# The last feed-forward product with tokens in the rows: what a change of layout in the final stage of an fp32 two-block transformer kernel does to its time

## The chip, the cores and the metric

The kernel runs on one core of one Trainium2 chip. The metric is device time in microseconds (us); of several runs the median is given. A profile is one execution recorded by the hardware profiler: its span reaches from the first to the last instruction. TensorE is called PE (its weight loads PEld), VectorE DVE, ScalarE ACT, GpSimd POOL, SyncE SP.

## What is computed

256 tokens of 1024 features pass through a first block of two layers (block-sparse attention, gated linear attention, attention into a memory), then 16 learned tokens are put ahead of them and a second block of two layers follows. Each layer of the second block is a feed-forward, a mixer and another feed-forward, each with a norm before and after. What the change touches is the last line of the loop at i = 1, and the return:

```python
def swiglu(h, w1, w3, w2):
    return (jax.nn.silu(h @ w1) * (h @ w3)) @ w2
...
        f = swiglu(rmsnorm(h, ffn_norm_pre[i, 1]), ffn_w1[i, 1], ffn_w3[i, 1], ffn_w2[i, 1])
        h = h + 0.5 * rmsnorm(f, ffn_norm_post[i, 1])
    return h[:, N_META:]
```

`w1` and `w3` are 1024 x 2816, `w2` is 2816 x 1024. All is float32.

## The kernel before

Activations lie with features in the partitions: `h[k]` is 128 features by 272 tokens (16 + 256), k = 0 to 7. A product takes a 128 x 128 block of weights as the stationary operand and streams the tokens past it (272 columns, or 256 where the 16 extra tokens aren't needed, as in the last feed-forward, `lo = 16`). For precision each operand is split into two fp32r parts, hi and lo, and `mm3` (L250) makes three matmuls of one product: lo by hi, hi by lo, hi by hi (L253, L254, L255).

The weights come in the order of one long plan (`full_plan`), eight blocks (a "chunk", 512 KB) to a DMA on SP's queue; ACT casts a chunk to its hi part (L222) and DVE subtracts to get the lo part (L223). Six chunks are held. `take` hands out blocks and lets the next chunk be loaded. A scheduler of the framework then sets the order of the instructions on each engine and puts the waits in.

`ffn` (L958): the first NG = 3 pairs of columns of w1 and w3 are made together with the eight k outside, since `h` becomes ready one k after another; the other 19 pairs follow one by one (`dense`, L478). `act` makes silu(a) * b of each and splits it into `fh[m]`, `fl[m]`, m = 0 to 21. Then the w2 product: for each of eight feature tiles m, 22 blocks by three matmuls of 256 columns into one PSUM bank; `branch_out` (L930) squares the bank on ACT (`fq`, L938), makes a copy times the gain on DVE (`fg`, L939) and sums squares on POOL (L948). After the last tile, matmuls with a matrix of 1/1024 (L956) put the mean of the squares of each token into all partitions.

The end of `second_block` (L1213 to L1222) takes Ln and Exp of that (`t_last`, `s_last`), and for each of the eight tiles a multiplication and an addition of `h` (two tiles on POOL, six on DVE) and a store of 128 KB, by turns from ACT's and SP's queues.

Between a mixer and a feed-forward stands `boundary` (L880): per k, `fg` times the scale (L892), the addition to `h` (L893, L895), the split into `xh[k]` (ACT, L352) and `xl[k]` (DVE, L353), a square on ACT (`sq`, two buffers) and a sum of squares on POOL (`acc`, L904). PE waits there for the first `xh`.

Of the kernel before, what the change touches and what calls it, by code (L numbers as in the profile page):

```python
# [8 lines left out]
F32 = mybir.dt.float32  # L9
# [58 lines left out]
DEFER = 12  # L68
AFTER_K = 3
# [38 lines left out]
def plan_ffn(i, j):  # L108
# [8 lines left out]
    p += plan_cols("ffn_w2_2", (i, j), [128 * m for m in range(KD)], KF)  # L117
# [49 lines left out]
class Kern:  # L167
# [82 lines left out]
    def mm3(self, out, a, b, start, stop):  # L250
        """out += a.T @ b from the two parts of each."""
# [5 lines left out]
    def mm3s(self, outs, ws, x, start, stop):  # L257
        """mm3 of several weight blocks with one x, its first part first."""
# [8 lines left out]
    def psum(self, **tags):  # L267
        """Shares out PSUM's banks: each tag's tiles follow one another in trace order."""
# [73 lines left out]
    def rsqrt(self, out, src, eps, n, tmp):  # L342
        """out = (src + eps) ** -0.5"""
        self.nc.scalar.activation(tmp, src, AF.Ln, bias=eps, scale=1.0)
        self.nc.scalar.activation(out, tmp, AF.Exp, bias=0.0, scale=-0.5)
# [9 lines left out]
    def sumsq(self, src, pool, n, tag, eng, qtag="sq"):  # L355
        """sum over the tiles of src of their squares, one tile."""
# [68 lines left out]
    def headnorm(self, dst, src, g):  # L425
        """dst = src * g / rms over each head's features."""
# [9 lines left out]
    def group_norm(self, tiles, gains):  # L436
        """Each of up to four tiles (two heads of 64 features each) over its heads' rms, times its gain."""
# [29 lines left out]
    def sigmoid(self, x):  # L467
        """exp(min(x, 0) - ln(1 + exp(-|x|))), silu's factor of x, by the tables that the norms use."""
# [16 lines left out]
    def mem_kv(self, l):  # L485
        """Keys (not normalised yet) and values of the memory tokens."""
# [26 lines left out]
    def first_layer(self, l):  # L513
# [13 lines left out]
        # inputs of the linear attention  # L527
# [28 lines left out]
        # queries and keys  # L556
# [200 lines left out]
    def gla(self, l, rb, qb, kb, vb):  # L757
# [24 lines left out]
        # states before chunks 1..3  # L782
# [16 lines left out]
        # scores by halving: the exponents never exceed 0  # L799
# [10 lines left out]
        # diagonal: q.k of each token  # L810
# [10 lines left out]
        def prepare(n):  # L821
# [5 lines left out]
            # queries of the four heads side by side, each head's features alone  # L827
# [52 lines left out]
    def boundary(self, fg, pss, g, after, lo=0, cols=False):  # L880
        """Adds the normalised branch to the residual and prepares the next product; returns the scale per
        token that the product carries."""
# [47 lines left out]
    def branch_out(self, ps, m, gpost, c, lo, st, bias=None, direct=1):  # L930
        """Evacuates feature tile m of a branch: its gained copy and its squares."""
# [26 lines left out]
    def ffn(self, i, j, scale, lo=0):  # L958
# [3 lines left out]
        with self.psum(mm=7), self.tc.tile_pool(name=self.nm("ffn"), bufs=1, reuse_waits="tile") as fp:  # L962
# [21 lines left out]
            for m in range(NG, KF):  # L984
                pa = self.dense("ffn_w1_2", self.xh, self.xl, n, KD, lo)
                pb = self.dense("ffn_w3_2", self.xh, self.xl, n, KD, lo)
                act(m, pa, pb)
# [290 lines left out]
```

## Time and profile before

| | |
|---|---|
| median of 3 runs | 1297.11 us (1296.04 to 1300.18) |
| profiled execution, span | 1289.3 us |
| its own time | the page gives no more than the span; the median lies 7.8 us above it |
| PE busy | 1253.6 us, 97% of the span |
| DVE, ACT, POOL busy | 66%, 54%, 17% |
| mean granted clock of PE | 0.992 |
| HBM read, written | 199.64 MB, 1.05 MB |

The busy time of PE is an upper bound of its work, since matmuls are pipelined and their ends are modelled; what a matmul costs is the distance between the starts of two in a row.

### The profile page before, as it was taken

The page shows a single profiled execution, that of the slowest core. Times are in us where ns is not written, and L with a number is a line of the kernel's source. Part 1 is how long each engine was busy: PE and PEld are TensorE (multiplying, and loading weights), DVE is VectorE, ACT ScalarE, POOL GpSimd, SP SyncE. Part 2 cuts the span into 40 slices and gives each one's busy share as a digit, 9 for nine tenths or more (in the row PEclk, how much of TensorE's full clock was granted, in tenths as well). Part 3 has the DMA queues.
Part 4 walks back from the last instruction along what each step waited for, and adds up shares of the span by engine and source line. Part 5 has one row for each costly group of instructions (what it writes and reads, how often), then busy time and mean ns, then how long its engine had stood idle before and what let it go on. Part 6 is the DMA issues. An engine that isn't in the chain of part 4 may idle for free.

```text
span 1289.3 us, 24664 instructions
## 1 busy us (share of the span) xinstructions
PE 1253.6 (97%) x9812; PEld 1203.9 (93%) x9812; DVE 855.6 (66%) x1431; ACT 694.8 (54%) x1207; POOL 216.3 (17%) x325
## 2 busy tenths in 40 slices
PE   8999999999999999799999999999999999999996
PEld 7888998889999999599999989999999888999996
DVE  7977768677666644786665477665466786866643
ACT  6768657486544443564444465444355665654541
POOL 5101110011311102441111022110120002311111
PEclk9999999999999999899999999999999999999999
DMA  8453553235555555146555536555536333665541
GB/s 297 141 172 106 166 165 99 101 128 169 176 181 178 174 173 178 33 158 186 169 177 179 175 115 205 177 179 169 177 100 194 131 99 99 211 190 188 181 146 34
DMA packets 59955, 202.29 MB, mean 157 GB/s; under 512 B 7488, under 2 KB 11584, under 8 KB 59840
## 3 DMA queue, kind: packets, MB, share of 16 engines
q1 hardware_dynamic: 59264, 200.19, 48.6%
q8 instruction: 77, 1.26, 0.4%
q10 hardware_dynamic: 576, 0.52, 0.1%
q14 instruction: 38, 0.31, 0.1%
HBM read 199.64 MB, written 1.05 MB: 156 GB/s over the span
## 4 chain that ended last, share of the span: by engine, by line
PE 89%; DVE 3%; ACT 2%; issue 1%; POOL 0%; DVEq 0%; ACTq 0%; POOLq 0%
PE mm L253 24%; PE mm L255 24%; PE mm L254 24%; PE mm L261 2%; PE mm L264 2%; PE mm L262 2%; DVE xl L353 1%; PE mb L253 1%; PE mb L255 1%; PE mb L254 1%; DVE fg L892 1%; PE gl L839 1%; DVE h L895 1%; PE mb L445 1%; PE at L1121 1%
## 5 line engine op out<-in xcount | busy, mean ns | idle before, releaser
L223 DVE TENSOR_TENSOR lo<-raw,hi 128x1024 fp32r<-128x1024 f32 (+1 forms) x376 | 471.9, 1259 | 255.9 <-ACT hi L222 255.2
L222 ACT CAST hi<-raw 128x1024 fp32r<-128x1024 f32 (+1 forms) x376 | 391.0, 1043 | 378.7 <-PE mm L255 353.4
L253 PE MATMUL mm<-xh,lo 128*128 128x272 f32 (+1 forms) x1680 | 484.8, 289 | 0.0
L255 PE MATMUL mm<-xh,hi 128*128 128x272 f32 (+1 forms) x1680 | 481.7, 287 | 0.0
L254 PE MATMUL mm<-xl,hi 128*128 128x272 f32 (+1 forms) x1680 | 481.1, 286 | 0.0
L253 PEld LDWEIGHTS mm<-xh,lo 128*128 128x128 f32 x1680 | 317.0, 189 | 4.2 <-issue 3.6
L254 PEld LDWEIGHTS mm<-xl,hi 128*128 128x128 f32 x1680 | 317.1, 189 | 1.2 <-issue 1.0
L255 PEld LDWEIGHTS mm<-xh,hi 128*128 128x128 f32 x1680 | 317.2, 189 | 0.4 <-issue 0.3
L255 PE MATMUL mm<-fh,hi 128*128 128x272 f32 (+1 forms) x704 | 201.8, 287 | 0.0
L253 PE MATMUL mm<-fh,lo 128*128 128x272 f32 (+1 forms) x704 | 201.4, 286 | 0.0
L254 PE MATMUL mm<-fl,hi 128*128 128x272 f32 (+1 forms) x704 | 201.0, 286 | 0.0
L973 POOL TENSOR_TENSOR a<-a,b 128x272 f32<-128x272 f32 (+1 forms) x88 | 82.8, 943 | 403.2 <-DVE b L972 367.6
L253 PEld LDWEIGHTS mm<-fh,lo 128*128 128x128 f32 x704 | 132.6, 188 | 0.0
L254 PEld LDWEIGHTS mm<-fl,hi 128*128 128x128 f32 x704 | 132.5, 188 | 0.0
L255 PEld LDWEIGHTS mm<-fh,hi 128*128 128x128 f32 x704 | 132.3, 188 | 0.0
L948 POOL TENSOR_TENSOR facc<-facc,fq 128x272 f32<-128x272 f32 (+1 forms) x34 | 31.8, 934 | 322.8 <-ACT fq L938 316.6
L972 DVE TENSOR_TENSOR b<-mm,r 128x272 f32<-128x272 f32 (+1 forms) x88 | 38.3, 435 | 42.6 <-PE mm L255 42.5
L348 ACT CAST fh<-a 128x272 fp32r<-128x272 f32 (+1 forms) x88 | 36.7, 417 | 54.2 <-POOL a L973 54.2
L261 PE MATMUL mm<-xh,lo 128*128 128x272 f32 (+1 forms) x208 | 55.7, 299 | 9.8 <-ACT xh L352 9.8
L262 PE MATMUL mm<-xh,hi 128*128 128x272 f32 (+1 forms) x208 | 54.2, 290 | 0.0
L261 PEld LDWEIGHTS mm<-xh,lo 128*128 128x128 f32 x208 | 40.1, 193 | 11.3 <-ACT xh L352 11.1
L349 DVE TENSOR_TENSOR fl<-a,fh 128x272 fp32r<-128x272 f32 (+1 forms) x88 | 39.0, 443 | 17.3 <-ACT fh L348 17.3
(347 smaller groups left out, 1697.5 us busy)
## 6 DMA issues: line engine op xcount, KB each, us to landing
raw<-in_w_dram SPq DMA_DIRECT2D x372, 512.0 KB, 3.5
h<-in_xt_dram SPq DMA_DIRECT2D x8, 128.0 KB, 5.5
raw<-in_w_dram SPq DMA_DIRECT2D x4, 256.0 KB, 5.8
memt<-in_memt_dram SPq DMA_DIRECT2D x1, 1024.0 KB, 8.5
memt<-in_memt_dram SPq DMA_DIRECT2D x2, 512.0 KB, 4.8
out_dram<-fg ACTq DMA_DIRECT2D x4, 128.0 KB, 1.8
out_dram<-fg SPq DMA_DIRECT2D x4, 128.0 KB, 1.8
vec<-in_vecs_dram SPq DMA_DIRECT2D x1, 336.5 KB, 3.0
```

Source lines behind the costliest of these rows:

```text
L222: nc.scalar.copy(hi[:, s], raw[:, s])
L223: nc.vector.tensor_sub(lo[:, s], raw[:, s], hi[:, s].bitcast(F32))
L253: mm(out, a[1], b[0], start=start, stop=False)
L254: mm(out, a[0], b[1], start=False, stop=False)
L255: mm(out, a[0], b[0], start=False, stop=stop)
L261: mm(out, w[1], x[0], start=start, stop=False)
L262: mm(out, w[0], x[0], start=False, stop=False)
L348: self.nc.scalar.copy(hi, x)
L349: self.nc.vector.tensor_sub(lo, x, hi.bitcast(F32))
L948: nc.gpsimd.tensor_add(R(st["acc"]), R(st["acc"]), R(q))
L972: nc.vector.tensor_mul(b, pb[:, :n], r[:, lo:])
L973: nc.gpsimd.tensor_mul(a, a, b)
```

## The change

The w2 product of the last feed-forward, and it alone, is turned over. The stationary operand is now a 128 x 128 piece of the activations (tokens by features of the middle layer), and 512 columns of weights are streamed past it, so that the result has 128 tokens in the partitions and 512 features in one PSUM bank. There are two halves of the features (b) and two of the tokens (t); in the second half of the features the last four of the 22 steps of k are made for t = 0 first and then for t = 1. The norm after it, the residual and the store follow in that layout: ACT squares with a running sum, DVE multiplies by the gain (a row spread over all partitions, `grow`, loaded by a new DMA and halved on POOL), Ln and Exp work on one column, and one instruction per 128 x 512 piece multiplies by the scale and adds the residual. The residual is `h` transposed by PE, 16 transposes of 128 x 128 in four groups behind the pairs m = 8, 10, 12 and 14, each group copied to SBUF by ACT. The output leaves in four stores of 256 KB. The weights' plan orders the same blocks of w2 to fit; the host passes one more array and no longer transposes the result. Instructions of the changed kernel have line numbers of their own (`mm3` stands at L259 to L261, the split of the weights at L228 and L229).

```diff
+    if (i, j) == (1, 1):
+        for n in range(2):
+            for k in range(KF):
+                p += block("ffn_w2_2", (i, j), k, 512 * n, 512)
+    else:
+        p += plan_cols("ffn_w2_2", (i, j), [128 * m for m in range(KD)], KF)
...
                 act(m, pa, pb)
+                if idx == (1, 1) and m in (8, 10, 12, 14):
+                    self.residual_rows(fp, (m - 8) // 2, lo)
             self.table("natural_log_exp_and_others")
+            if idx == (1, 1):
+                return self.last_rows(fp, fh, fl, lo)
...
+    def residual_rows(self, fp, q, lo):
+        nc = self.nc
+        if q == 0:
+            self.hT = [fp.tile([128, D], F32, name=f"hT{t}") for t in range(2)]
+            self.grow = fp.tile([128, D], F32, name="grow")
+            nc.sync.dma_start(self.grow, self.io["grow"].to_broadcast([128, D]))
+            nc.gpsimd.tensor_scalar(self.grow, self.grow, 0.5, None, op0=OP.mult)
+        b, t = divmod(q, 2)
+        ps = self.bank()
+        for i in range(4):
+            nc.tensor.transpose(ps[:, 128 * i:128 * i + 128], self.h[4 * b + i][:, lo + 128 * t:lo + 128 * t + 128],
+                                self.ident)
+        nc.scalar.copy(self.hT[t][:, 512 * b:512 * b + 512], ps)
...
+    def last_rows(self, fp, fh, fl, lo):
...
+        for b in range(2):
+            c = slice(512 * b, 512 * b + 512)
+            acc = [self.bank() for _ in range(2)]
+            x = lambda t, k: [p[k][:, lo + 128 * t:lo + 128 * t + 128] for p in (fh, fl)]
+            held = KF - LAST_K if b else KF
+            for k in range(held):
+                w = self.take(4, "ffn_w2_2")
+                for t in range(2):
+                    self.mm3(acc[t], x(t, k), w, k == 0, k == KF - 1)
+            ws = [self.take(4, "ffn_w2_2") for k in range(held, KF)]
+            for t in range(2):
+                for k, w in zip(range(held, KF), ws):
+                    self.mm3(acc[t], x(t, k), w, k == 0, k == KF - 1)
+                sq = fp.tile([128, 512], F32, name=self.nm("sqr"), tag="sqr", bufs=2)
+                nc.scalar.activation(sq, acc[t], AF.Square, accum_out=ss[:, 2 * t + b:2 * t + b + 1])
+                f = fg[t][b] = fp.tile([128, 512], F32, name=self.nm("fgr"), tag=f"fgr{t}{b}")
+                nc.vector.tensor_mul(f, acc[t], self.grow[:, c])
+                if b == 0:
...
+                    continue
+                s = ss[:, 6 + t:7 + t]
+                nc.scalar.activation(s, ss[:, 2 * t + 1:2 * t + 2], AF.Ln, bias=ss[:, 4 + t:5 + t], scale=1.0 / D)
+                nc.scalar.activation(s, s, AF.Exp, bias=0.0, scale=-0.5)
+                for d in range(2):
+                    o = fg[t][d]
+                    e = slice(512 * d, 512 * d + 512)
+                    nc.vector.scalar_tensor_tensor(o, o, s, self.hT[t][:, e], op0=OP.mult, op1=OP.add)
+                    (nc.sync if d else nc.scalar).dma_start(self.io["out"][t][:, e], o)
...
-            st = self.ffn(1, 1, r, lo=NMETA)
-            s = t2.tile([128, L2], F32, name="s_last", tag="s")[:, NMETA:]
-            t = t2.tile([128, L2], F32, name="t_last", tag="ms")[:, NMETA:]
-            self.rsqrt(s, st["pss"][:, NMETA:L2], self.eps, S, t)
-            for k in range(KD):
-                f = st["fg"][k][:, NMETA:]
-                eng = nc.gpsimd if k in (2, 5) else nc.vector
-                eng.tensor_mul(f, f, s)
-                eng.tensor_add(f, f, self.h[k][:, NMETA:])
-                (nc.sync if k % 2 else nc.scalar).dma_start(self.io["out"][k], f)
+            self.ffn(1, 1, r, lo=NMETA)
```

**Where the scheduler puts the load and the halving of `grow`.** In the code they stand behind the pair m = 8. On POOL's queue at the `boundary` ahead of the last feed-forward (`facc` are the sums of the attention's branch, `acc` the sums of the boundary) stood before:

```order
L948 TENSOR_TENSOR facc_12935<-facc_12935,fq_13083 128x256 [waits Activation_49,Pool_49]
L948 TENSOR_TENSOR facc_12935<-facc_12935,fq_13088 128x256 [waits Activation_49,Pool_49]
L904 TENSOR_TENSOR acc_13131<-acc_13131,sq_13141 128x256 [waits PE_49,Activation_49]
L904 TENSOR_TENSOR acc_13131<-acc_13131,sq_13148 128x256 [waits Activation_49,Pool_49]
L904 TENSOR_TENSOR acc_13131<-acc_13131,sq_13155 128x256 [waits Activation_49,Pool_49]
```

and now, with SP's queue of the same place behind it (`raw` are the chunks of weights):

```order
L954 TENSOR_TENSOR facc_12935<-facc_12935,fq_13083 128x256 [waits Activation_49,Pool_49]
L954 TENSOR_TENSOR facc_12935<-facc_12935,fq_13088 128x256 [waits Activation_49,Pool_49]
L1012 TENSOR_SCALAR grow<-grow 128x1024 [waits DMAHW4_49,DVE_49]
L910 TENSOR_TENSOR acc_13131<-acc_13131,sq_13141 128x256 [waits PE_49,Activation_49]
L910 TENSOR_TENSOR acc_13131<-acc_13131,sq_13148 128x256 [waits Activation_49,Pool_49]
L910 TENSOR_TENSOR acc_13131<-acc_13131,sq_13155 128x256 [waits Activation_49,Pool_49]
```

```order
L222 DMA raw_13338<-in_w_dram 128x1024 [waits DMAHW4_49,DVE_49]
L222 DMA raw_13362<-in_w_dram 128x1024 [waits DMAHW5_49,DVE_49]
L1011 DMA grow<-in_grow_dram 128x1024 [waits PE_49,Pool_49]
L222 DMA raw_13393<-in_w_dram 128x1024 [waits DMAHW6_49,DVE_49,Activation_49]
L222 DMA raw_13460<-in_w_dram 128x1024 [waits DMAHW7_49,DVE_49,Activation_49]
```

The load has moved ahead of the chunks of the feed-forward, and the halving ahead of the sums of the boundary.

**The end on ACT and DVE.** On DVE's queue behind the last split of weights there stood before fifteen rows: `fg` of three tiles, and six multiplications and six additions (POOL had the other two of each); the last eight were:

```order
L1220 TENSOR_TENSOR fg_2571_15138<-fg_2571_15138,s_last 128x256
L1220 TENSOR_TENSOR fg_2583_15228<-fg_2583_15228,s_last 128x256
L1221 TENSOR_TENSOR fg_2571_15138<-fg_2571_15138,h_76 128x256 [waits DVE_49]
L1221 TENSOR_TENSOR fg_2583_15228<-fg_2583_15228,h_77 128x256 [waits DVE_49]
L1220 TENSOR_TENSOR fg_2598_15390<-fg_2598_15390,s_last 128x256
L1220 TENSOR_TENSOR fg_2601_15462<-fg_2601_15462,s_last 128x256
L1221 TENSOR_TENSOR fg_2598_15390<-fg_2598_15390,h_79 128x256 [waits DVE_49]
L1221 TENSOR_TENSOR fg_2601_15462<-fg_2601_15462,h_80 128x256 [waits DVE_49]
```

Now all that DVE has there, t = 0 and then t = 1 (`mm_15030` and `mm_15031` are the two banks):

```order
L1041 TENSOR_TENSOR fgr_15190<-mm_15030,grow 128x512 [waits Activation_49]
L1052 SCALAR_TENSOR_TENSOR fgr_15022<-fgr_15022,ss_rows,hT_13879 128x512 [waits DVE_49,Activation_49]
L1052 SCALAR_TENSOR_TENSOR fgr_15190<-fgr_15190,ss_rows,hT_13879 128x512 [waits DVE_49]
L1041 TENSOR_TENSOR fgr_15212<-mm_15031,grow 128x512 [waits Activation_49]
L1052 SCALAR_TENSOR_TENSOR fgr_15027<-fgr_15027,ss_rows,hT_13880 128x512 [waits Activation_49]
L1052 SCALAR_TENSOR_TENSOR fgr_15212<-fgr_15212,ss_rows,hT_13880 128x512 [waits DVE_49]
```

and on ACT, where the store of t = 0 stands ahead of the Square of t = 1:

```order
L1039 ACTIVATE sqr_15188,ss_rows<-mm_15030 128x512 [waits PE_49,Activation_49]
L1047 ACTIVATE ss_rows<-ss_rows 128x1 [waits DVE_49,Activation_49]
L1048 ACTIVATE ss_rows<-ss_rows 128x1 [waits Activation_49]
L1053 DMA out_dram<-fgr_15022 128x512 [waits DVE_49]
L1039 ACTIVATE sqr_15210,ss_rows<-mm_15031 128x512 [waits PE_49,Activation_49]
L1047 ACTIVATE ss_rows<-ss_rows 128x1 [waits Activation_49]
L1048 ACTIVATE ss_rows<-ss_rows 128x1 [waits Activation_49]
L1053 DMA out_dram<-fgr_15027 128x512 [waits DVE_49]
```

So behind the last matmul three DVE instructions follow a Square, where twelve followed the Exp; and the ACT queue now holds a store that waits for DVE ahead of the last Square.

## Rows read from the trace of the kernel before

**Rows 1.** The page, part 4: shares of the span in the chain that ended last, by engine.

```profile
PE 89%; DVE 3%; ACT 2%; issue 1%; POOL 0%; DVEq 0%; ACTq 0%; POOLq 0%
```

**Rows 2.** Busy time by engine in the stretch of the last w2 product: stretch, its length, then per engine busy us and count, PE's granted clock, DMA share, GB/s.

```profile
1215.00:1277.50 62.50, 62.50 (x530) 62.50 (x530) 24.82 (x26) 22.02 (x26) 6.33 (x7) 1.00 0.32 102
```

**Rows 3.** Groups by line and shape: one of the three lines of `mm3` in that product; the other two have as many.

```profile
L255 PE MATMUL mm<-fh,hi 128*128 128x256 f32 x176 | 49.6, 282 | 0.0
```

**Rows 4.** PE's instructions in order of time (start, duration, both us): the first and the last of the 528 matmuls of that product.

```profile
1215.29 0.28 PE L253 MATMUL mm<-fh,lo 128*128 128x256 f32 x1
...
1277.68 0.28 PE L255 MATMUL mm<-fh,hi 128*128 128x256 f32 x1
```

**Rows 5.** The same view in the second layer of the first block, where a product with 512 columns of weights moving past activations exists already (values of its attention): first and last of two runs of eleven matmuls without a break.

```profile
254.09 0.40 PE L254 MATMUL mm<-lo,xh 128*128 128x512 f32 x1
...
256.42 0.39 PE L255 MATMUL mm<-hi,xh 128*128 128x512 f32 x1
...
257.93 0.39 PE L254 MATMUL mm<-lo,xh 128*128 128x512 f32 x1
...
260.21 0.40 PE L255 MATMUL mm<-hi,xh 128*128 128x512 f32 x1
```

**Rows 6.** The same view in the attention of the second block: five transposes between two fp32r products.

```profile
1057.04 0.28 PE L255 MATMUL mm<-oh,hi 128*128 128x256 f32 x1
1057.16 0.49 PE L1141 MATMUL at<-ident,e 128*128 128x128 f32 x3
1057.49 0.38 PE L1143 MATMUL at<-ident,e 128*16 128x128 f32 x2
...
1057.95 0.28 PE L255 MATMUL mm<-oh,hi 128*128 128x256 f32 x1
```

**Rows 7.** The chain that ended last, at its end (start, length, what), and behind it, from the instructions in order of time, the issue of the last store.

```profile
1278.05 0.39 ACT fq L938
...
1280.18 1.29 DVE fg L1220 x2
...
1285.73 0.34 DVE fg L1221
...
1286.43 0.33 SPq L1222 DMA_DIRECT2D out_dram<-fg  x1
```

**Rows 8.** Groups by line and shape on ACT: count, then busy us and mean ns of one, then idle time before them. The second is a Square from PSUM, the third what follows each instruction with a running sum.

```profile
L744 ACT COPY pT<-mb 128x512 f32<-128x512 f32 x8 | 4.5, 599 | 1.0 <-PE mb L741 1.0
L938 ACT ACTIVATE fq<-mm 128x256 f32<-128x256 f32 x10 | 3.7, 384 | 20.9 <-PE mm L255 20.9
L688 ACT ACTIVATION_READ_ACCUMULATOR lg<-lg,sm 128x1 f32 x32 | 6.0, 186 | 0.0
L877 ACT ACTIVATE rt<-ss,eps 128x2 f32<-128x2 f32 x1 | 0.3, 262 | 1.7 <-PE ss L919 1.7
L878 ACT ACTIVATE rc<-rt 128x2 f32<-128x2 f32 x1 | 0.2, 193 | 0.0
```

**Rows 9.** The same on DVE, two shapes of 512 columns.

```profile
L829 DVE TENSOR_TENSOR bd<-X,hm 128x512 f32<-128x512 f32 x12 | 8.2, 683 | 0.0
L474 DVE SCALAR_TENSOR_TENSOR sl<-ga,sl 128x512 f32<-128x512 f32 x8 | 6.1, 762 | 2.0 <-ACT sl L473 2.0
```

**Rows 10.** The page, part 6: DMA issues, KB each, median us from issue to landing.

```profile
raw<-in_w_dram SPq DMA_DIRECT2D x372, 512.0 KB, 3.5
...
out_dram<-fg SPq DMA_DIRECT2D x4, 128.0 KB, 1.8
```

**Rows 11.** Instructions in order of time at the `boundary` ahead of the last feed-forward: DVE, ACT and PE up to the first matmul, and DVE beside POOL a little later.

```profile
1086.84 0.42 DVE L892 TENSOR_TENSOR fg<-fg,s 128x256 f32<-128x256 f32 x1 [1.23 <-ACT s L878]
1087.30 0.43 DVE L893 TENSOR_TENSOR h<-h,fg 128x256 f32<-128x256 f32 x1
...
1087.76 0.51 ACT L352 ACTIVATE xh<-h,vec 128x256 fp32r<-128x256 f32 x1 [0.95 <-DVE h L893]
...
1088.32 0.39 PE L261 MATMUL mm<-xh,lo 128*128 128x256 f32 x1 [2.47 <-ACT xh L352]
...
1090.05 1.61 POOL L904 TENSOR_TENSOR acc<-acc,sq 128x256 f32<-128x256 f32 x2 [5.66 <-ACT sq L903]
1090.10 0.97 DVE L895 TENSOR_TENSOR h<-h,fg 128x256 f32<-128x256 f32 x1
```

**Rows 12.** Busy time by engine just behind that first matmul, columns as in rows 2.

```profile
1088.30:1092.40 4.10, 4.08 (x22) 4.09 (x23) 4.10 (x10) 3.09 (x8) 1.87 (x3) 0.59 0.02 4
```

**Rows 13.** SP's two issues of chunks that stand on either side of the new load, and DVE's split of the chunk of the second.

```profile
1081.23 0.33 SPq L216 DMA_DIRECT2D raw<-in_w_dram  x1
...
1096.77 0.33 SPq L216 DMA_DIRECT2D raw<-in_w_dram  x1
...
1106.73 1.23 DVE L223 TENSOR_TENSOR lo<-raw,hi 128x1024 fp32r<-128x1024 f32 x1 [0.80 <-ACT hi L222]
```

**Rows 14.** The only multiplications by a constant on POOL, in the first microseconds of the kernel (group), and one DVE addition ahead of them and one beside them, in order of time.

```profile
L339 POOL TENSOR_SCALAR alibi<-d 128x256 f32<-128x256 f32 x8 | 7.8, 990 | 0.3
...
10.97 0.42 DVE L365 TENSOR_TENSOR acc<-acc,sq 128x256 f32<-128x256 f32 x1
...
12.79 0.62 DVE L365 TENSOR_TENSOR acc<-acc,sq 128x256 f32<-128x256 f32 x1
```

**Rows 15.** Groups by line in the stretch 1215.3 to 1277.5: ACT's casts of weights, and what they waited for.

```profile
L222 ACT CAST hi<-raw 128x1024 fp32r<-128x1024 f32 x17 | 17.8, 1049 | 22.0 <-PE mm L255 22.0
```

More of the change, by code (lines that the diff above doesn't have):

```diff
@@ L68 @@
 DEFER = 12
+LAST_K = 4
 AFTER_K = 3
@@ L116, in plan_ffn @@
         p += plan_cols("ffn_w3_2", (i, j), (128 * m,), KD)
-    p += plan_cols("ffn_w2_2", (i, j), [128 * m for m in range(KD)], KF)
+    if (i, j) == (1, 1):
[4 more added lines that the diff above has]
+        p += plan_cols("ffn_w2_2", (i, j), [128 * m for m in range(KD)], KF)
     return p
@@ new lines, in last_rows @@
+    def last_rows(self, fp, fh, fl, lo):
+        nc = self.nc
+        ss = fp.tile([128, 8], F32, name="ss_rows")
+        fg = [[None] * 2 for _ in range(2)]
+        for b in range(2):
[16 more added lines that the diff above has]
+                if b == 0:
+                    nc.vector.tensor_scalar(ss[:, 4 + t:5 + t], ss[:, 2 * t:2 * t + 1], 1.0 / D, EPS, op0=OP.mult,
+                                            op1=OP.add)
+                    continue
[7 more added lines that the diff above has]
+                    (nc.sync if d else nc.scalar).dma_start(self.io["out"][t][:, e], o)
@@ L1258, in pack @@
         "metat": fm(A["meta_tokens_2"]),
+        "grow": A["ffn_norm_post_2"][1, 1].reshape(1, D),
     }
@@ L1271 @@
         io[name] = nc.dram_tensor(f"in_{name}_dram", a.shape, mybir.dt.from_np(a.dtype), kind="ExternalInput").ap()
-    io["out"] = nc.dram_tensor("out_0_dram", (KD, 128, S), F32, kind="ExternalOutput").ap()
+    io["out"] = nc.dram_tensor("out_0_dram", (2, 128, D), F32, kind="ExternalOutput").ap()
     with _tile.TileContext(nc) as tc:
@@ L1276 @@
     got = r.results[0]["out_0_dram"]
-    return np.ascontiguousarray(np.asarray(got).reshape(D, S).T).reshape(1, S, D)
+    return np.asarray(got).reshape(1, S, D)
```

## The prediction

> **What bounds the kernel now.** I read the shares of the chain that ended last first: 89% of it is PE [rows 1]. So a saving counts only where PE is busy, or where PE waits. Next come the stages. Over the last w2 product PE has no pause, and DVE and ACT work 25 and 22 of 62.5 us [rows 2]; their splits of weights wait for PE, not PE for them [rows 15]. There are 528 matmuls [rows 3], and from the first start to the last are 62.4 us [rows 4], so each takes 62.39/527 = 0.118 us. The duration in such a row (0.28) is latency and prices nothing. Then the end: after the start of the last matmul at 1277.68 the kernel still runs 11.6 us, and the chain there is a Square, matmuls with the mean, Ln, Exp, and six us of DVE, from 1280.18 to 1286.07 [rows 4, 7]. Here PE is idle and everything counts. Last, the boundary ahead of this feed-forward, since the scheduler has put new work there: PE waits for two DVE instructions and one of ACT, until 1288.32 [rows 11].
>
> The profiled span is 1289.3 us, the median of the runs 7.8 us more; I take these 7.8 us as unchanged and count from 1297.1. A measurement of this kernel can tell about 0.3% (3.9 us) from no change.
>
> **1. The product.** 528 matmuls of 256 columns become 264 of 512: as many columns in all. What a matmul of 512 columns takes, with weights moving and activations stationary, stands in the trace: ten steps from 254.09 to 256.42, and ten from 257.93 to 260.21 [rows 5], 0.233 and 0.228. Two of 256 columns take 0.237. I take 0.231, the middle: from first to last start 263 x 0.231 = 60.8 us, **-1.6 us**. Bounds: -2.4 at 0.228, -0.1 at 0.237. Chunks of weights are then wanted every 2.77 in place of 2.84 us; the casts have 22 us of waiting to spare [rows 15], so I cost that at nothing. The first half's Squares and multiplications run beside the second half's matmuls, as `fq` and `fg` did.
>
> **2. The transposes.** 16 of them lie on PE's path. Five in a row put 1057.95 - 1057.04 = 0.91 us between matmuls that otherwise stand three steps, 0.354, apart [rows 6]: 0.111 each, the change from one kind to the other included. 16 x 0.111 = **+1.8 us**. The row's durations (0.49 for three started 0.11 apart, so 0.27 for one) are latency again; if the change paid them it would be 4.4. The lower bound is the same 1.8: the work is new and PE has no gap. The Trainium skill (TensorE: Matmul & The Clock Gate, Part 4: PE-mode transpose) gives about 275 ns for one in a kernel's context; by that figure the estimate would be 4.4 us, the upper bound above. The rows agree with it as a latency and not as a price. ACT's four copies of 512 columns, 0.60 each [rows 8], lie in a stretch where PE isn't waited on by them: the bank they free is wanted seven products later.
>
> **3. The end.** Now, counted from the start T of the last matmul. Before, the Square began 0.37 later [rows 4, 7]; 512 columns stream 0.11 longer, 0.48. A Square of 256 columns takes 0.38, a copy of 512 takes 0.60: I take 0.62, and 0.19 for reading the sum out [rows 8]: T + 1.29. The multiplication by the gain waits for the Square, as `fg` did for `fq`: start at T + 1.33. Ln and Exp on one column (0.26 + 0.19, [rows 8]) lie beside it. DVE then has 0.68 + 0.76 + 0.76 [rows 9], less 0.08 for each overlap of two in a row: T + 3.4. The store of 256 KB lands between the 1.8 us of 128 KB and the 3.5 of 512 KB [rows 10]; by size 2.4: T + 5.8. From the last landing to the end of the span were 1289.3 - 1286.43 - 1.8 = 1.1 us [rows 7, 10]: T + 6.9, against 11.6. **-4.7 us**, with bounds of -5.3 and -3.6 from the two landings. The half t = 0 ends 12 matmuls, 2.8 us, earlier; its store stands on ACT's queue ahead of the last Square and waits for DVE's second instruction: 1.29 + 0.04 + 0.60 + 0.76 = 2.7 us after t = 0's last matmul, and issuing takes 0.33 [rows 7], so ACT is free at about T + 0.2 to 0.3, before T + 0.48. It hides, by 0.2 us.
>
> The eight Squares, `fg` and the sums on POOL of the old product go, and were hidden under PE [rows 2]: nothing.
>
> **4. The boundary.** Load and halving of `grow` stand earlier than in the code. On SP the load stands between the chunks issued at 1081.23 and 1096.77 [rows 13]; the second chunk has another reason for its late issue, so the queue loses nothing. With 3.5 us for 512 KB [rows 10], and a chunk ahead of it in the same queue, `grow` lands between 1085.1 and about 1088.5. POOL then multiplies 1024 columns: four times the 0.99 us of 256 [rows 14] is 4 us at most. It can meet the two DVE instructions on PE's path, 1086.84 to 1087.73 [rows 11]. Beside POOL's multiplications by a constant one DVE addition took 0.62 in place of 0.42 [rows 14]. I take one such 0.2: **+0.2 us**. The lower bound is 0, when `grow` lands after 1087.7: the next instructions have some 2 us of slack, since PE's clock is then at 0.59 of full on average [rows 12], between its levels of 1.2 and 2.4 GHz, and it works off the first k slowly. The upper bound is the first rival.
>
> **Sum:** -1.6 + 1.8 - 4.7 + 0.2 = -4.3 us, 1297.1 - 4.3 = **1292.8 us**. With the bounds of points 1 and 3 this case runs from 1291.4 to 1295.4.
>
> **The rivals.** *DVE is locked out while POOL halves `grow`.* Beside POOL's sums the addition of DVE took 0.97 in place of 0.42: begun at 1090.10, it ended just after POOL's first sum did [rows 11]. If the halving holds DVE off for as long as it runs, 4 us, and begins at 1086.2, DVE's first instruction begins at 1090.2 in place of 1086.84: +3.3 us, 1295.9. For it speak the sums; against it the multiplications by a constant, beside which DVE lost only 0.2 [rows 14], and the chance that `grow` comes too late to matter. The Trainium skill (SBUF — State Buffer, Who interferes with whom) has this as its rule: a DVE instruction with two SBUF inputs and a GpSimd instruction that reads SBUF exclude each other for the whole instruction. The sums of rows 11 agree with that rule, the additions of rows 14 don't. Chance 0.17.
>
> *The transposes are not pipelined* in the midst of this product and cost their latency: +2.6, 1295.4. Against it: they are pipelined between products of the same kind in rows 6. Chance 0.07.
>
> *The stream gains more.* At 0.228 a matmul and a landing of 1.8 us the sum is -5.9: 1291.2. Chance 0.13.
>
> *SP's queue is blocked, and it is slower.* The load of `grow` waits for PE and for POOL. Were the event it waits for one of this feed-forward, in place of one long past, the loads of all its chunks would stand behind it. That decides from the point where the wait outlasts 1096.77 by the spare time of the next chunk, which lands 3.5 us after its issue and is split at 1106.73 [rows 10, 13]: 6.5 us, so from 1103.3. If it waited for its place in the code, behind the pair m = 8 (six pairs of 48 matmuls at 0.118 after PE's first 144, about 1141), PE would lose 38 us: 1335. Against it: the tiles that lay in that memory belong to stages that are over, and the scheduler placed the load ahead of the feed-forward's own. Chance 0.02.
>
> *The change does not do what it says*: 512 columns take exactly twice 256 and the stores land late, so that -0.1 + 1.8 - 3.6 + 0.2 = -1.7 is left: 1295.4. Chance 0.03.
>
> **How the numbers follow.** The forecast has 0.58. Of it a little under two thirds lies under 1293.2, the 0.3% line, which is only 0.4 us away; the faster rival lies there whole: 0.37 + 0.13, and a little of the others, 0.52 for faster. The lock, the dear transposes and the rest of the forecast make 0.45 for no change. Slower by over 0.3% is the blocked queue, with a little for what I don't see: 0.03. The range of 8 in 10 goes from 1290.5 (below the faster rival, by what a median of few runs may lie off) to 1296.2 (above the lock).
>
> **What the profile after would show.** Steps of 0.231 between starts in the w2 product, and about 60.8 us from first to last; four groups of transposes, each holding the next product back by 0.44; from the last matmul to the end of the span 6.9 us, with Square, multiplication and two more DVE instructions in it; `grow`'s halving on POOL between 1085 and 1092, and PE's first matmul of the feed-forward at 1088.5. The forecast is wrong if that first matmul comes after 1090 (the lock), if the steps lie at 0.237 or more, if the last store lands over 3 us after its issue, or if the last Square begins late because ACT still holds the store of t = 0.

## The result and the profile after

The changed kernel takes 1288.49 us (median of 22 runs, 1286.42 to 1297.19) beside 1295.43 for the kernel before (22 runs, 1290.84 to 1300.88): a ratio of 0.9949 [0.9935, 0.9963], so 4.8 to 8.4 us less. The forecast was 1292.8, the range from 1290.5: the sign is right, the time lies 2 us under the range. Where that comes from is followed below: the sum of what the change does in the traces is the one forecast (two of its terms were off and cancelled), and the point it was counted from was not.

The profiled execution of the changed kernel has a span of 1295.5 us and a time of 1297.2, the longest of the 22. So the spans of this profile and of the one before can't be subtracted. Stretches of the two can, where PE's granted clock (the share of its full speed that PE was allowed) is the same. The engines and the chain, from the page:

```profile
PE 1263.2 (98%) x9560; PEld 1200.7 (93%) x9560; DVE 850.9 (66%) x1421; ACT 696.3 (54%) x1213; POOL 214.7 (17%) x316
PE 90%; DVE 2%; ACT 2%; issue 1%; POOL 0%; DVEq 0%; ACTq 0%; POOLq 0%
```

DVE has 2% of the chain where it had 3 [rows 1], as a shorter end would have it; PE's 90% in place of 89 also holds the longer half clock of this execution. The product (PE in order of time: its first and last matmul, then the group of one of its three lines):

```profile
1228.20 0.39 PE L259 MATMUL mm<-hi,fl 128*128 128x512 f32 x1
...
1289.24 0.39 PE L261 MATMUL mm<-hi,fh 128*128 128x512 f32 x1
```

```profile
L261 PE MATMUL mm<-hi,fh 128*128 128x512 f32 x88 | 34.6, 393 | 0.0
```

These answer to [rows 3, 4]: 264 matmuls in 61.03 us, 0.232 a step, where 528 took 62.38. **-1.35 us.** One of the four groups of transposes, in the same view:

```profile
1152.49 0.28 PE L261 MATMUL mm<-xh,hi 128*128 128x256 f32 x1
1152.61 0.60 PE L1016 MATMUL mm<-ident,h 128*128 128x128 f32 x4
1152.96 0.36 PE L259 MATMUL mm<-xh,lo 128*128 128x256 f32 x1
1153.16 0.28 PE L260 MATMUL mm<-xl,hi 128*128 128x256 f32 x1
```

From 1152.49 to 1153.16 are 0.67 us; two steps of 0.118 would be 0.24. So a group costs 0.43 to 0.44, and four cost **+1.76 us** (all four groups are alike). The last 924 matmuls ahead of the product say the same: 109.24 us before, 111.00 after. The end, DVE, ACT and SP in order of time, and the stores from the page:

```profile
1290.38 0.69 DVE L1041 TENSOR_TENSOR fgr<-mm,grow 128x512 f32<-128x512 f32 x1 [0.72 <-ACT sqr L1039]
1290.99 1.41 DVE L1052 SCALAR_TENSOR_TENSOR fgr<-fgr,ss_rows,hT 128x512 f32<-128x512 f32 x2
...
1289.04 0.38 ACTq L1053 DMA_DIRECT2D out_dram<-fgr  x1
1289.66 0.60 ACT L1039 ACTIVATE sqr<-mm 128x512 f32<-128x512 f32 x1 [1.48 <-DVE fgr L1052]
1290.16 0.19 ACT L1039 ACTIVATION_READ_ACCUMULATOR sqr<-mm 128x1 f32 x1
```

```profile
out_dram<-fgr SPq DMA_DIRECT2D x2, 256.0 KB, 2.1
```

Counted from the last matmul, T = 1289.24: Square at T + 0.42, multiplication at T + 1.14, DVE done at T + 3.16 (1290.99 + 1.41), the store issued then lands 2.1 us later, and the span ends at T + 6.24. ACT's wait ahead of the Square is put down to DVE, but ACT had issued t = 0's store by 1289.42: the last matmul set it. Before, it was 11.62 [rows 4, 7]: **-5.38 us.**

Part of that lay in how the kernel before shared its end between DVE and POOL. Two of DVE's additions beside POOL's, and two without:

```profile
1281.39 1.81 DVE L1221 TENSOR_TENSOR fg<-fg,h 128x256 f32<-128x256 f32 x2
1282.01 1.76 POOL L1221 TENSOR_TENSOR fg<-fg,h 128x256 f32<-128x256 f32 x2
...
1285.66 0.75 DVE L1221 TENSOR_TENSOR fg<-fg,h 128x256 f32<-128x256 f32 x2
```

Four of the twelve DVE instructions were lengthened so, by about 0.53 us each, 2.1 in all, while POOL took four instructions off DVE that would have cost it some 0.34 each. By this estimate the old end could have been about 0.8 us shorter with DVE alone; no run tried it.

Last, the boundary (POOL, DVE, PE, and the load's row of the page):

```profile
1096.07 2.77 POOL L1012 TENSOR_SCALAR grow<-grow 128x1024 f32<-128x1024 f32 x1 [2.08 <-DMA grow<-in_grow_dram]
1096.44 0.94 DVE L898 TENSOR_TENSOR fg<-fg,s 128x256 f32<-128x256 f32 x1 [1.23 <-ACT s L884]
1097.41 0.42 DVE L899 TENSOR_TENSOR h<-h,fg 128x256 f32<-128x256 f32 x1
1097.76 0.75 DVE L898 TENSOR_TENSOR fg<-fg,s 128x256 f32<-128x256 f32 x2
...
1098.43 0.58 PE L267 MATMUL mm<-xh,lo 128*128 128x256 f32 x1 [2.99 <-ACT xh L358]
```

```profile
grow<-in_grow_dram SPq DMA_DIRECT2D x1, 512.0 KB, 4.7
```

The multiplication that took 0.42 [rows 11] takes 0.94, and PE's gap, from the last fp32r product's last matmul to the first of the feed-forward, is 4.50 us in place of 3.99. **+0.5 us** here; over five profiles of this kernel 4.50, 4.67, 4.74, 4.83 and 4.70, so +0.7 on average.

Sum over the stretches: -1.35 + 1.76 - 5.38 + 0.7 = -4.3 us.

### The profile page after: what moved, and what is told of

Read it like the earlier page. It is cut to its first block, busy times and chain, and to the rows that moved or that the text cites. A ratio compares the mean times of both kernels' runs of the same rounds, so it can differ in the third digit from the quotient of the medians.

```text
span 1295.5 us, 24140 instructions
## 1 busy us (share of the span) xinstructions
PE 1263.2 (98%) x9560; PEld 1200.7 (93%) x9560; DVE 850.9 (66%) x1421; ACT 696.3 (54%) x1213; POOL 214.7 (17%) x316
## 4 chain that ended last, share of the span: by engine, by line
PE 90%; DVE 2%; ACT 2%; issue 1%; POOL 0%; DVEq 0%; ACTq 0%; POOLq 0%
PE mm L259 24%; PE mm L261 24%; PE mm L260 23%; PE mm L267 2%; PE mm L268 2%; PE mm L270 2%; PE mb L259 1%; PE mb L260 1%; PE mb L261 1%; PE gl L845 1%; DVE xl L359 1%; PE mb L451 1%; PE at L1181 1%; PE ss L962 1%; DVE fg L898 1%
## 5 line engine op out<-in xcount | busy, mean ns | idle before, releaser
L229 DVE TENSOR_TENSOR lo<-raw,hi 128x1024 fp32r<-128x1024 f32 (+1 forms) x376 | 470.7, 1255 | 259.6 <-ACT hi L228 259.0
L228 ACT CAST hi<-raw 128x1024 fp32r<-128x1024 f32 (+1 forms) x376 | 391.2, 1043 | 384.7 <-PE mm L261 356.2
L259 PE MATMUL mm<-xh,lo 128*128 128x272 f32 (+1 forms) x1680 | 485.6, 289 | 0.0
L261 PE MATMUL mm<-xh,hi 128*128 128x272 f32 (+1 forms) x1680 | 481.8, 287 | 0.0
L259 PEld LDWEIGHTS mm<-xh,lo 128*128 128x128 f32 x1680 | 317.5, 189 | 4.2 <-issue 3.6
L261 PEld LDWEIGHTS mm<-xh,hi 128*128 128x128 f32 x1680 | 317.2, 189 | 0.4 <-issue 0.3
L261 PE MATMUL mm<-fh,hi 128*128 128x272 f32 x528 | 152.4, 289 | 0.0
L259 PE MATMUL mm<-fh,lo 128*128 128x272 f32 x528 | 152.1, 288 | 0.0
L260 PE MATMUL mm<-fl,hi 128*128 128x272 f32 x528 | 151.8, 287 | 0.0
L259 PEld LDWEIGHTS mm<-fh,lo 128*128 128x128 f32 x528 | 99.6, 189 | 0.0
L260 PEld LDWEIGHTS mm<-fl,hi 128*128 128x128 f32 x528 | 99.5, 188 | 0.0
L261 PEld LDWEIGHTS mm<-fh,hi 128*128 128x128 f32 x528 | 99.3, 188 | 0.0
L954 POOL TENSOR_TENSOR facc<-facc,fq 128x272 f32<-128x272 f32 (+1 forms) x28 | 26.1, 934 | 277.4 <-ACT fq L944 267.5
L910 POOL TENSOR_TENSOR acc<-acc,sq 128x272 f32<-128x272 f32 (+1 forms) x35 | 41.9, 1197 | 57.0 <-ACT sq L909 55.9
```

The lines of the kernel that those rows point to most:

```text
L228: nc.scalar.copy(hi[:, s], raw[:, s])
L229: nc.vector.tensor_sub(lo[:, s], raw[:, s], hi[:, s].bitcast(F32))
L259: mm(out, a[1], b[0], start=start, stop=False)
L260: mm(out, a[0], b[1], start=False, stop=False)
L261: mm(out, a[0], b[0], start=False, stop=stop)
L910: nc.gpsimd.tensor_add(R(acc), R(acc), R(q))
```

## The experiments

**What is open.** The medians differ by 6.9 us, the stretches by 4.3. Theory A: the stretches are all, and the rest is how long PE happened to run at half clock in the executions that were drawn. Theory B: something is missed, or the change itself spares PE half clock. In the runs below, the ratio is always to runs of the kernel before that were made beside them (the reference runs). The first four:

*The kernel before again.* No edit.

> The kernel before, unchanged, with its own profile and the granted clock of each run. What is open: the medians differ by 6.9 us (interval 4.8 to 8.4), the quickest runs by 4.4, and the terms seen in the two traces (product -1.35, transposes +1.76, end -5.38, boundary +0.5 to +1.5) sum to between -4.5 and -3.5. Theory A: the terms are all there is, and the rest is how often stretches at half clock fall into an execution: then the runs of this kernel differ from one another by the clock (lower mean clock, longer time), ratio 1.000 within 0.002, and the quickest run of the kernel after lies 3.5 to 5 us under the quickest here. Theory B: a term is missed, every run of the kernel after is shorter by about 7 us at the same clock. In the trace both expect 62.4 us for the last product and 11.6 us from its last matmul to the end; theory B expects another difference of over 1 us at a place that is the same in both profiles of this kernel.

Measured: 1292.86, ratio to the reference runs of the same program 0.9984 [0.9962, 1.0007]. The end 11.61, the product 62.38, the gap 3.99, as in the first profile. So the stretches repeat to 0.02 us, and the time of one program does not: its two sets of runs have medians 2 us apart (12 runs and 35). Each run has its mean granted clock, and the runs follow it: 1289.69 at 0.993, 1298.85 at 0.986. The quickest run of the changed kernel lies 3.3 us under the quickest here, a little less than theory A's 3.5 to 5.

*Without the halving.*

```
-            nc.gpsimd.tensor_scalar(self.grow, self.grow, 0.5, None, op0=OP.mult)
...
-  nc.vector.tensor_scalar(ss[:, 4 + t:5 + t], ss[:, 2 * t:2 * t + 1], 1.0 / D, EPS, op0=OP.mult,
+  nc.vector.tensor_scalar(ss[:, 4 + t:5 + t], ss[:, 2 * t:2 * t + 1], 4.0 / D, 4 * EPS, op0=OP.mult,
...
-  nc.scalar.activation(s, ss[:, 2 * t + 1:2 * t + 2], AF.Ln, bias=ss[:, 4 + t:5 + t], scale=1.0 / D)
+  nc.scalar.activation(s, ss[:, 2 * t + 1:2 * t + 2], AF.Ln, bias=ss[:, 4 + t:5 + t], scale=4.0 / D)
```

> The changed kernel without POOL's halving of grow: the factor 0.5 goes into Ln's scale and bias (4/D and 4 times eps), the load stays where it is. If the halving held up DVE's first multiplication of the boundary (0.94 in place of 0.42 us), that instruction takes 0.42 again, PE's first matmul of the feed-forward comes 0.5 us earlier against the end of the product before it, and the time is 0.5 us less than the kernel after, up to 1.5 if the longer stretch at half clock came from it too: 1287.0 to 1288.0 where the kernel after has 1288.5. If the load of 512 KB is what disturbs the boundary, nothing changes.

Measured: 1288.29, ratio 0.9955 [0.9937, 0.9974]. The same place on DVE:

```profile
1088.94 0.42 DVE L898 TENSOR_TENSOR fg<-fg,s 128x256 f32<-128x256 f32 x1 [1.22 <-ACT s L884]
1089.40 0.43 DVE L899 TENSOR_TENSOR h<-h,fg 128x256 f32<-128x256 f32 x1
```

The gap is 3.99 again. So the halving costs 0.5 to 0.85 us there and the load nothing. The time is that of the changed kernel (1288.49) and could not show it alone.

*Without the transposes.*

```
-            self.hT = [fp.tile([128, D], F32, name=f"hT{t}") for t in range(2)]
...
+            self.hT = [self.grow] * 2
...
-        ps = self.bank()
-        for i in range(4):
...
-        nc.scalar.copy(self.hT[t][:, 512 * b:512 * b + 512], ps)
```

> The changed kernel without the 16 transposes and ACT's four copies; the last addition takes grow in place of the residual, so the residual is left out of the output. By the forecast's price (0.111 each) 1.8 us less than the kernel after: 1286.7. If they cost their latency of 0.27 each, 4.4 less: 1284.1. If ACT's copies held back PE as well, more than 1.8 is missing in the steps around them.

Measured: 1289.86, ratio 0.9958 [0.9934, 0.9981]; the 924 matmuls ahead of the product take 109.24 us again. The transposes cost 1.76, the copies nothing. The time misses the expected 1286.7 and lies above the changed kernel's, at a mean clock of 0.9890 beside 0.9910: the median alone decides nothing (at the same clock, see below).

*Two matmuls of 256 for each of 512.*

```
+    def mm3h(self, out, a, b, start, stop):
+        if start:
+            return self.mm3(out, a, b, start, stop)
+        for c in (slice(0, 256), slice(256, 512)):
+            self.mm3(out[:, c], a, [p[:, c] for p in b], False, stop and c.start > 0)
...
-                    self.mm3(acc[t], x(t, k), w, k == 0, k == KF - 1)
+                    self.mm3h(acc[t], x(t, k), w, k == 0, k == KF - 1)
```

> The changed kernel with its matmuls of 512 columns cut into two of 256 each (all but the 12 of the first k), everything else the same. If the gain of the product is in the number of matmuls, 252 x (2 x 0.1183 - 0.2321) = 1.1 us more than the kernel after, 1289.6, and 62.2 us from first to last. The rival: the step per column is the same for both widths and the shorter product comes from something else (weight loads, fewer pauses): no change.

Measured: 1290.25, ratio 0.9961 [0.9939, 0.9983]; the product takes 62.25 us from first to last, as expected. The gain lies in the number of matmuls.

The next four:

*The changed kernel again.* No edit.

> The changed kernel, unchanged, on the same chip as this batch's runs of the kernel before. So far the runs of one kernel lie on a line against their mean granted clock, 0.9 us for each 0.001; the 22 runs of this kernel had 0.9910 on average, 35 of the kernel before 0.9872. Theory A (the terms, and the clock's stretches by chance): at one and the same clock outside the end it is 4 to 4.5 us under the kernel before; the median difference of this batch can be anything from 3 to 7 according to the clocks. Theory B (the change itself gives PE fewer stretches at half clock, or some term is missed): the mean clock is again 0.003 to 0.004 above that of the kernel before, and the medians are again 6 to 7 us apart. In the trace both expect a gap of 4.5 to 4.7 us between the last feed-forward's first matmul and the one before it where the kernel before has 3.99, and 6.2 us from the last matmul to the end.

Measured: 1289.33, ratio 0.9956 [0.9935, 0.9978], a median 7.5 us under that of the 28 reference runs, mean clock 0.9900 beside 0.9865. Gap 4.67, end 6.24. The clock speaks for B here; one pair of sets could not settle it, and it was drawn again (below).

*Both halves of the tokens together* (`LAST_K = 4` becomes 0).

> The changed kernel with LAST_K = 0: both halves of the tokens walk through every k together and end 0.7 us apart instead of 2.8. DVE then has the multiplication and two additions of both halves after the last matmul: from T + 0.44, twice 2.0 us, T + 4.5 in place of T + 3.2. The end from the last matmul grows from 6.2 to 7.5 us, and the time by 1.3. The rival: the store's landing hides it (two stores at once land later anyway, or ACT's queue is in the way): no change, or over 2.

Measured: 1291.30, ratio 0.9958 [0.9935, 0.9981]; the end takes 7.93 us, 1.7 more than with 4 and 0.4 more than expected: DVE does both multiplications first, then all four additions in a row.

```profile
1290.26 2.73 DVE L1052 SCALAR_TENSOR_TENSOR fgr<-fgr,ss_rows,hT 128x512 f32<-128x512 f32 x4
```

So holding four k back for one half is worth 1.7 us of the end's 5.4.

*The halving in four* (four multiplications of 256 columns on POOL).

> The changed kernel with POOL's halving of grow as four instructions of 256 columns. In three profiles the halving (2.8 to 3.0 us on POOL) lengthened just one DVE instruction, by 0.5 to 0.7 us, the one that ran when POOL began, and the next ones were as short as ever while POOL still worked. If each POOL instruction holds up DVE once at its start, three or four DVE instructions are longer by about 0.5 each, and the gap ahead of the first matmul grows from 4.5-4.7 to 5.0 or more (only two DVE instructions stand on that path). If only a first access after a rest costs, one instruction is longer and the gap stays.

Measured: one run, 1289.32, gap 3.99. Neither expectation is met: the two DVE instructions on the path are as short as ever (0.42, 0.43) though POOL had begun 0.33 us ahead of them; behind them one DVE instruction in each of the later three pieces takes 0.61 or 0.62.

*A shorter end*, with the halving out as above; `turned` does the four transposes into a bank and returns it.

```
+        if t == 0:
+            nc.scalar.copy(self.hT[0][:, 512 * b:512 * b + 512], self.turned(b, t, lo))
...
-        nc.scalar.copy(self.hT[t][:, 512 * b:512 * b + 512], ps)
...
+                if b and t:
+                    rows = [self.turned(d, t, lo) for d in range(2)]
...
-                for d in range(2):
...
+                for d, a, z in ((0, 0, 512), (1, 0, 256), (1, 256, 512)) if t else ((0, 0, 512), (1, 0, 512)):
```

> A version meant to beat both: the changed kernel without the halving (the 0.5 in Ln's scale and bias), with the 8 transposes of the second half of the tokens put behind the last matmul, where PE is idle and DVE adds them straight from PSUM (no copy), and the last addition and its store cut into two of 256 columns. Expected from the runs so far: -0.55 at the boundary, 8 x 0.11 = -0.9 in PE's stream, -0.2 at the end (128 KB land in 1.8 in place of 2.05 us, for 0.06 more on DVE): 1.6 us less than the kernel after at the same clock, 6.0 us from the last product's matmul to the end. The rival: the transposes come too late for DVE (8 x 0.11 after the last matmul is before the additions at T + 1.75, unless they cost their latency of 0.27 each, then T + 2.4 and the end is 0.6 longer), or an addition that reads PSUM is slower.

Measured: 1288.81, ratio 0.9940 [0.9916, 0.9964]. Gap 3.99, the matmuls ahead of the product 110.12 (-0.88), the end 6.38 (+0.14). PE, DVE and the stores at the end:

```profile
1277.26 1.03 PE L1019 MATMUL mm<-ident,h 128*128 128x128 f32 x8
...
1278.79 1.52 DVE L1058 SCALAR_TENSOR_TENSOR fgr<-fgr,ss_rows,mm 128x512 f32<-128x512 f32 x3
```

```profile
out_dram<-fgr ACTq DMA_DIRECT2D x1, 128.0 KB, 2.0
```

The transposes are done before DVE asks for them, as expected. Cutting the last addition fails: DVE needs 1.52 in place of 1.41, and 128 KB land in 2.0, hardly sooner than 256 KB in 2.1.

Then two copies of either program beside one another:

*Kernel before, changed kernel, kernel before, changed kernel.* No edits.

> The kernel before, unchanged, one of four runs that stand beside one another and beside the reference runs of this batch, all of the same two programs. What is open: over all runs so far the kernel before has a mean clock of 0.9873 and the kernel after and its variants 0.990; a shorter stretch of half clock behind the last matmul explains 0.0012 of that (about 3.2 us less of it), the rest would be worth some 1.5 us. Theory A: the rest is chance in the draw; the copies of either program scatter by as much among themselves as the two programs differ, beyond 0.0012 and the terms of 4 to 4.5 us. Theory B: the changed program draws fewer stretches; then both of its copies have a mean clock above both copies of this one by 0.003, and the medians lie 6 to 7 us apart. For this copy A expects 1292.5 to 1297, a mean clock of 0.987 to 0.990; B 1295 to 1297, 0.987.

> The changed kernel, unchanged, beside the copies of the kernel before. Theory A: a median of 1288 to 1292, mean clock 0.988 to 0.992, and 4 to 4.5 us less than the copies of the kernel before once the clock is counted out. Theory B: 1288 to 1290, mean clock 0.990 to 0.991, above both copies of the kernel before.

> A second copy of the kernel before. Theory A: its mean clock may lie up to 0.002 from that of the first copy and from the reference runs. Theory B: within 0.001 of both, 0.987.

> A second copy of the changed kernel. Theory A: its mean clock may lie up to 0.002 from that of the first copy, on either side. Theory B: within 0.001 of it, 0.990 to 0.991. In all four traces: 11.6 us from the last matmul to the end before, 6.2 after; a gap ahead of the last feed-forward of 3.99 before and 4.5 to 4.7 after.

| | median | ratio to 35 reference runs | mean clock |
|---|---|---|---|
| before, a | 1296.26 | 1.0005 [0.9982, 1.0028] | 0.9878 |
| after, a | 1293.18 | 0.9988 [0.9968, 1.0008] | 0.9885 |
| before, b | 1294.10 | 1.0009 [0.9990, 1.0028] | 0.9882 |
| after, b | 1288.74 | 0.9975 [0.9958, 0.9992] | 0.9903 |
| reference (before) | 1292.91 | | 0.9888 |

Theory B falls in the form in which it was put, 6 to 7 us apart and a clock 0.003 higher: here one copy of the changed kernel has the clock of the kernel before (and a median above what either theory expected), and the gain by the ratios is 1.5 and 3.2 us, not 6.9. The gaps are 3.98 in both copies before, 4.74 and 4.83 after. What the clock does is seen in one stretch that the change doesn't touch, around the pooled mixer, 508 to 577 us (columns as in [rows 2]; in turn the first profile before, copy b before, the first profile after, copy a after):

```profile
508.00:577.00 69.00, 60.02 (x424) 54.97 (x424) 53.34 (x88) 40.41 (x77) 34.85 (x81) 0.95 0.31 104
```

```profile
508.00:577.00 69.00, 60.06 (x362) 53.56 (x361) 48.10 (x79) 36.28 (x69) 30.71 (x78) 0.83 0.24 80
```

```profile
508.00:577.00 69.00, 60.23 (x360) 53.35 (x359) 47.78 (x78) 36.30 (x69) 30.36 (x78) 0.83 0.23 80
```

```profile
508.00:577.00 69.00, 60.15 (x420) 55.09 (x419) 52.77 (x87) 40.16 (x76) 31.79 (x81) 0.95 0.30 100
```

In 69 us at the same busy time PE does 424 or 420 matmuls at 0.95 of the clock, and 362 or 360 at 0.83, whichever the program. In the two at 0.83, PE ran 23.9 us at 0.5 (1.2 GHz in place of 2.4), 17.1 of them on end, begun 1.5 and 2.4 us behind a wait of PE of 1.4 us; in the two at 0.95 it ran 6.8. There PE had waited at the same place too (1.4 and 0.8 us) and kept its full clock, so the wait alone doesn't decide it; what does was not found.

Now all 151 runs before and 59 after whose clock is known: medians 1294.5 and 1289.1, means 1295.5 and 1290.4 (5.1 us apart, give or take 1.0). A straight line of time against mean clock, with one slope for all kernels (0.92 us for each 0.001), puts the changed kernel 3.0 us (2.6 to 3.5) under the kernel before at the same mean clock. Against the changed kernel it puts the run without transposes 1.6 us lower, the one without the halving 1.1 lower and the one with two matmuls of 256 0.8 higher, each give or take 0.9; the traces say 1.8, 0.7 and 1.2. The mean clock counts half clock behind the last matmul too, where PE has no work left that the end waits for: 5.7 to 6.5 us of the span in four profiles before, 1.1 to 3.8 in five after, on average 3.1 us less, 0.0012 of the mean clock, 1.1 us by the slope. So 4.1 us at the same clock of the working stretches, beside 4.3 from the traces. Of the 5.1, some 1.0 goes with the clock of the working stretches. That is no more than the doubt of the 5.1 itself: it may be the draw, and a small share of the change in it is not excluded.

The last four are one version with many runs and three single profiled executions, two without the halving (the edit shown above) and one of the changed kernel:

*A shorter end without the cut addition* (the version above with additions and stores of 512 columns).

> The shorter version without the cut of the last addition (which lost 0.14 us at the end): no halving, the second half's 8 transposes behind the last matmul, additions and stores of 512 columns. From the last matmul to the end 6.24 us as in the kernel after; 0.88 us less in the stream of w1 and w3; the gap ahead of the feed-forward 3.99. Together 1.6 us (0.88 and 0.70) less than the kernel after at the same clock, and 5.9 less than the kernel before. If the longer gap of the kernel after also brings a second stretch at half clock, this version has one stretch of 3.4 us there, not 6.8.

> One more profile without the halving. So far, behind the gap ahead of the last feed-forward, half clock lasted 6.8 us in five of seven profiles with the halving (gap 4.5 to 4.8) and in none of six with the gap at 3.99 and no POOL work beside it (5 times 3.4, once none). If the longer gap is the cause, it is 3.4 or none here; if it is chance, 6.8 can come here as well.

> One more profile of the changed kernel: a gap of 4.5 to 4.85 us. If the gap is the cause of the longer stretch, 6.8 us of half clock behind it in most profiles; if chance, 3.4.

> As the other look without the halving: 3.4 us or none if the gap decides, either if chance does.

The first: 1291.03, ratio 0.9951 [0.9930, 0.9972]; gap 3.99, 110.12 us ahead of the product, end 6.19: 0.7 + 0.88 + 0.05 = 1.6 us less than the changed kernel in the traces, as expected. By time the two can't be told apart (at the same clock it lies 1.0 us lower, with some 0.9 of doubt). So in the stretches named it beats both kernels, and by its measured time only the kernel before.

The single executions: 1288.41 and 1285.87 without the halving, 1297.91 for the changed kernel. Behind the gap, half clock lasted 3.4 us in both of the former and 6.8 in the latter; but 6.8 in the profile of the shorter version as well, whose gap is 3.99. Over all profiles that is 6.8 in six of eight with one halving of 1024 columns, in one of nine without it, and in the one with the halving in four. That the halving makes the longer stretch likelier is suggested and not shown; it stays open.

## Why the prediction was right and wrong

**The starting point failed**: "the median of the runs 7.8 us more; I take these 7.8 us as unchanged and count from 1297.1". What lies around the span is 1.7 us (1297.2 - 1295.5 after, and 1.7 to 1.8 in every run that has both). So the profiled execution, with its span of 1289.3, was one of 1291.0, near the quick end, and 1297.1 was the middle of three draws. The other 6.1 us are put down to half clock that the profiled execution didn't have: those three runs have no clock on record, but the 31 later runs of this kernel with a mean clock of 0.986, where the profile has 0.992, have a median of 1297.7. The kernel before has a median of 1294.5 over 151 runs, so the starting point was 2.6 us too high. The same step set the range too narrow: 0.7 us below the faster rival was no measure of a draw whose runs go from 1289.7 to 1302.5.

**Product: right** in kind, -1.35 for -1.6; the step was 0.232, not 0.231. *The stream gains more* (0.228) didn't come. (Its -5.9 leaves out the boundary's +0.2, and the blocked queue's 1335 leaves out the gain of 4.3; the forecast uses neither.)

**Transposes: right**, 1.76 for 1.8; *not pipelined* is refuted by the run without them. The Trainium skill (TensorE: Matmul & The Clock Gate, Part 4: PE-mode transpose) with about 275 ns holds here as a latency, as the row with 0.60 for four that start 0.11 apart shows.

**The end: right in its order, undersized**, -5.4 for -4.7. The last landing was 2.1 where 2.4 was worked out by size (0.3), the sum of squares was read out while the Square still ran (1290.16 within 1289.66 + 0.60, 0.1), and Square, additions and the way from the landing to the end were each 0.05 to 0.1 shorter. t = 0's store hid, as forecast.

**The boundary: right place, undersized**, +0.5 to +0.85 for +0.2. `grow` landed 4.7 us after its issue, so the halving began about when DVE did. *DVE is locked out* was half right. In all eight profiles with one halving of 1024 columns the DVE instruction that met it ended 1.3 us after POOL's start (once 1.5), whenever it had begun, and then DVE ran at full pace while POOL had another 1.4 to go. So the rule of the Trainium skill (SBUF — State Buffer, Who interferes with whom), exclusion for the whole instruction, does not hold for POOL's recorded span of 2.77 us here. As the DVE instruction takes 0.42 by itself, DVE was held off for some 0.9 us, the first third of that span (an estimate). The sign that was to show the lock, a first matmul after 1090, came about without it: the matmul stands at 1098.43, since this execution had by then lost 9.6 us more than the first profile before, to half clock (30.7 us of it beside 10.2) and to one wait of 1.67 us at 977.6. A gap counted from the matmul before it would have been the better sign.

**SP's queue** wasn't blocked (the 924 matmuls ahead of the product take nothing beyond the transposes), and **the change did what it says**.

The terms erred by +0.25, -0.04, -0.7 and +0.5. That these cancel, -4.3 forecast and -4.3 in the traces, is luck. From the right start that is 1290.2. The measured 1288.5 lies 1.7 lower, and that goes with the clock of these 22 runs: they have a mean clock of 0.9910; the kernel before with the shorter tail of half clock would have 0.9877 + 0.0012 = 0.9889; 0.0021 more at 0.92 us for each 0.001 is 1.9 us. The 37 later runs of the same program have 0.9894 and a median of 1289.5: drawn again, three quarters of that excess of clock were gone, so most of it was the draw.

## What to carry to other kernels

Before counting from a median, compare the profiled execution's own time (span and what lies around it) with the runs, and say which draw it was; where runs scatter by more than the change, the sum of the stretches is the measurement, and a copy of the same kernel beside itself shows what a median can tell. Putting the last product's tokens into rows pays at the end, not in the stream: what it saves in matmuls, the transposes of the residual take back. New work is best kept away from a boundary where PE waits: POOL's halving cost 0.5 to 0.85 us there, and the factor 0.5 fitted into Ln's scale for nothing.

## What the runs showed of the hardware

- Granted clock: PE runs at full or at half clock (0.5). From 500 us to the last matmul, half clock began within a wait of PE of 0.8 us or more, or up to 2.4 us behind one (once 10.6 us behind, in the second profile of the kernel before), but the same wait brings it in one execution and not in another. One program, the kernel before, has 14 us of it in one execution and over 35 in another, and the places repeat from program to program, mostly 518 to 527, 529 to 558, 750 to 763, 955 to 971 and 1088 to 1105 us.
- Beside POOL's multiplication by a constant over 1024 columns (2.77 us), one DVE instruction with two SBUF inputs did not end before 1.31 to 1.35 us after POOL's start in seven profiles of eight (1.54 in the other); over 256 columns (0.85 to 1.1 us, one profile) it cost DVE 0.2 us or less.
- Stores at the end: 128 KB landed in 1.8 us (eight stores, kernel before) and 2.0 (two stores, the shorter end), 256 KB in 2.1: twice the size cost at most 0.3 us.
